# Where the adaLN blocks, the first three FFN blocks and the last sums stand in a two-layer diffusion trunk

## The chip, the cores and the metric

The kernel runs on one core of a Trainium2 chip. The metric is the device time of one execution in microseconds (us). Six actors matter: TensorE (PE, matrix products and transposes), VectorE (DVE), ScalarE (ACT), GpSimd (POOL), SyncE (SP), which issues nearly all transfers, and the transfer queues behind SP.

## The reference, cut to what matters

Two layers over 256 latent and 256 context tokens of width 1024: layer 0 mixes tokens with a Conformer convolution, layer 1 with retention; each is followed by a SwiGLU FFN. Every sub-layer is normalised, modulated by adaLN vectors (shift, scale, gate) and added back through its gate.

```python
def modulate(x, g, shift, scale):
    return rms_norm(x, g) * (1 + scale) + shift
...
def conv_module(h, w1, b1, dw, dw_b, norm_g, w2):
    ...
    y = jax.nn.silu(layer_norm(y, norm_g))
    return y @ w2
...
def swiglu_ffn(h, w_gu, w_down):
    a, b = jnp.split(h @ w_gu, 2, axis=-1)
    return (jax.nn.silu(a) * b) @ w_down
...
        x = x + g_m * ox
        x = x + g_f * swiglu_ffn(modulate(x, norm_ffn[i], sh_f, sc_f), ffn_w_gu[i], ffn_w_down[i])
```

## The kernel before, in words

**Products.** Everything is fp32, but PE works on pairs of shorter parts: each operand is split into a high part (`wh`, `ah`) and a low part (`wl`, `al`), and a product is three matmuls (`mm3`): high by high, low by high, high by low. A weight piece comes by a 1 MB load into a `raw` buffer, ACT copies its high part (128x1024), and DVE, or for some pieces POOL, subtracts to get the low part. `raw` buffers are shared by many loads, so a load waits for whatever read the buffer last. An activation is made of transposes on PE into one of two PSUM tiles called `aux`, a modulation on ACT or DVE, a CAST (high part) and a subtraction (low part) on DVE.

**The convolution's last product (`w2`).** `z` has eight chunks of 128 features. For each chunk ACT and DVE make `z`, and PE runs the 12 matmuls of chunk k into the four sums `w_00` to `w_03` (the tokens' four tiles, first 512 columns). Then come `w_10` to `w_13`, the other 512 columns, one tile after the other, each over all eight chunks. Their weights are the loads `w2_10` and `w2_11`. Between them stand pieces of the adaLN product: `begin(i)` is 16 matmuls (`ada`), `evict(i)` copies the sums on ACT (`adasb`), `cols(i)` is four matmuls on that copy, and `finish(i)` reduces on DVE. From block 4 the gate row is made (`gr` on PE, `grow` on ACT, `grd` to DRAM and two broadcast loads `gate` back); the residuals of `w_0*` and `w_1*` wait for `gate`.

**Residual, squares, norm.** `residual` is two DVE operations of 128x512 (times the gate, plus `res`); `squares` (`sqj`) on ACT sums their squares; `normed_sq` turns the sums of a pair of tiles into `rstd` (a chain of small DVE operations, some on 128x2, some on 128x1) and scales `res` to `xn`. `norm_parts` is a generator: each step transposes two features' tiles, modulates and splits them. Stream 0 (`x0`) are the first 256 tokens, stream 1 (`x1`) the others.

**FFN.** Block j of 22 makes `fa` and `fb` (128 hidden features each, 512 tokens) with 48 matmuls. Blocks 0 and 1 run in halves of 256 tokens, since `h` of stream 1 is not ready when they begin. From block 2 on, a `silu(a)*b` on ACT and DVE follows each block, and `fill_rows` loads and sums the adaLN columns of the next sub-layers (`adat`, `crow`, `junk`).

**The end.** In layer 1 the context is only read, so the last FFN has two token tiles and four sums `y`; each is multiplied by the gate, added to `res` and stored, the last one in two halves of 256 columns.

**What sets the order.** The instruction order of each engine is found by a scheduler at build time, except where `pin` holds it in the order of the code. Some pieces sit at places given by small tables (`T3_W2`, `CTX_AT`).

Of the kernel before, what the change touches and what calls it, by code (L numbers as in the profile page):

```python
# [82 lines left out]
def trunk_kernel(ctx: ExitStack, tc, x_in, ctx_in, cond, small, consts, rope, dist, ada, ada4, adat,  # L83
# [202 lines left out]
    def normed_sq(tiles, also=lambda i: None, act=False):  # L286
# [550 lines left out]
    for ch in range(KC):  # L837
# [21 lines left out]
        if ch == 4:  # L859
            begin(5)  # L860
            evict(5)
        if ch == 6:
            cols(5)
            finish(5)
    w2r[1, 1] = load(w2[1, 1], name="w2_11", also=pin)

    def w2_order(n):
        return ([(t, k) for k in range(KC) for t in range(4)] if n == 0
                else [(t, k) for t in range(4) for k in range(KC)])
# [4 lines left out]
    for t, k in w2_order(0):  # L874
        tk = slice(P * t, P * t + P)
        mm3(pw[t], (z[0][:, k, tk], z[1][:, k, tk]), w(k), k == 0, k == KC - 1)
        if k == KC - 1:
            residual(t, 0, pw[t], gates[t // 2])
            squares(t, 0, PAIRS[t // 2])
# [2 lines left out]
    ads = ExitStack()
    ad = ads.enter_context(tc.tile_pool(name="ad", bufs=1))

    crow = ad.tile([P, 2, D], F32, name="crow")
    for s in range(2):
        pin(nc.sync.dma_start(crow[:, s, :], cond[0:1, D * s:D * s + D].to_broadcast([P, D])))
        nc.scalar.activation(crow[:, s, :], crow[:, s, :], AF.Silu)
    junk = ad.tile([P, D], F32, name="junk")
# [22 lines left out]
    for n in (1,):  # L912
        pw = [acc(f"w2_{n}{t}") for t in range(4)]
        split_w2(n, 0)
        split_w2(n, 1)
        w = kview(w2p[n, 0] + w2p[n, 1], 512)
        for t, k in w2_order(n):
            tk = slice(P * t, P * t + P)
            last = pin if n and t > 1 else (lambda i: None)
            mm3(pw[t], (z[0][:, k, tk], z[1][:, k, tk]), w(k), k == 0, k == KC - 1, last)  # L920
            if k == KC - 1:
                residual(t, n, pw[t], gates[t // 2], last)
                squares(t, n, PAIRS[t // 2], last)
            if n and (t, k) == (1, KC - 1):
                mod_scale(0, 1)
                h = new_act(pB, "h0f")
                x0 = normed_sq(PAIRS[0], pin)
            if n and t == 3:
                if k == 0:
                    parts = norm_parts(0, 1, 0, x0, h, 0, pin, pin, range(1, 8, 2))  # L930
                if k in T3_W2:
                    next(parts)
# [7 lines left out]
    def gu_products(j, w, pa, pb, c0, c1, parts=None):  # L940
        for g, dst in enumerate((pa, pb)):
            c = slice(128 * g, 128 * g + 128)
            for k in range(KC):
                mm3(dst[:, c0:c1], w(k, c), (h[0][:, k, c0:c1], h[1][:, k, c0:c1]), k == 0, k == KC - 1,
                    pin if parts else lambda i: None)
                if parts and (g, k) in CTX_AT:
                    next(parts)
# [578 lines left out]
```

## Time and profile before

| what | value |
|---|---|
| median of 3 runs | 1071.44 us (1071.35 to 1071.82) |
| the profiled execution | 1070.6 us, its span 1068.8 us |
| TensorE's granted clock, mean | 1.00 |
| PE busy | 1053.4 us, 99% of the span |
| DVE / ACT / POOL busy | 690.3 / 412.2 / 161.4 us |
| chain that ended last | PE 92%, DVE 5%, ACT 1% |

A busy PE is in matmuls that overlap each other, so the time of one is read from start to start and not from its own duration. What can be won lies where PE waits for another engine, and at the two ends of the program.

### The profile page before, as it was taken

How to read it: one execution, taken by the hardware profiler on the slowest of the kernel's cores; microseconds unless marked ns; L12 is line 12 of the kernel's file. 1: busy time of each engine (PE TensorE's matmuls, PEld its weight loads, DVE VectorE, ACT ScalarE, POOL GpSimd, SP SyncE). 2: the span in 40 equal slices, each digit the busy share in tenths (PEclk: the TensorE clock that was granted, in tenths of full speed). 3: DMA queues.
4: the chain of work that ended last, by engine and by line, in shares of the span. 5: the costliest groups of instructions: out<-in, count | busy, mean ns of one | idle time of the engine just before them, and what ended most of it. 6: DMA issues, size and time to landing. Idle time of an engine off the chain costs nothing.

```text
span 1068.8 us, 13292 instructions
## 1 busy us (share of the span) xinstructions
PE 1053.4 (99%) x5214; PEld 841.2 (79%) x5214; DVE 690.3 (65%) x1163; ACT 412.2 (39%) x582; POOL 161.4 (15%) x120
## 2 busy tenths in 40 slices
PE   8999999989999999999999999999999999999998
PEld 4666745888888888888888888888888877888886
DVE  5598865768999886455746886457454565555545
ACT  4565455433222222222323563333332464444442
POOL 0079743030000000000002510000000470000000
PEclk9999999999999999999999999999999999999999
DMA  9567766724666685524132532235233353555551
GB/s 377 198 219 272 263 241 261 315 80 158 223 222 257 229 304 192 186 82 182 52 118 79 198 126 111 86 131 197 79 120 118 118 193 142 186 175 190 197 193 44
DMA packets 35037, 190.13 MB, mean 178 GB/s; under 512 B 3936, under 2 KB 4640, under 8 KB 15776
## 3 DMA queue, kind: packets, MB, share of 16 engines
q1 hardware_dynamic: 34544, 188.01, 48.6%
q10 hardware_dynamic: 432, 1.28, 0.3%
q8 instruction: 41, 0.67, 0.2%
q14 instruction: 20, 0.16, 0.0%
HBM read 185.85 MB, written 3.42 MB: 177 GB/s over the span
## 4 chain that ended last, share of the span: by engine, by line
PE 92%; DVE 5%; ACT 1%; issue 1%; DMA 0%; SPq 0%; ACTq 0%; DVEq 0%
PE fa L193 4%; PE fa L194 4%; PE fa L192 4%; PE fb L193 4%; PE fb L194 4%; PE fb L192 4%; PE u L194 3%; PE u L193 3%; PE u L192 3%; PE cv L529 3%; PE v L192 3%; PE v L194 3%; PE dn L192 3%; PE dn L193 3%; PE v L193 3%; PE dn L194 3%
## 5 line engine op out<-in xcount | busy, mean ns | idle before, releaser
L163 DVE TENSOR_TENSOR wl_gu<-raw_gu,wh_gu 128x1024 fp32r<-128x1024 f32 x76 | 92.3, 1223 | 78.9 <-ACT wh_gu L155 78.2
L155 ACT ACTIVATE wh_gu<-raw_gu 128x1024 fp32r<-128x1024 f32 x80 | 83.8, 1058 | 132.6 <-PE fb L193 47.9
L900 DVE SCALAR_TENSOR_TENSOR junk<-raw_adat,crow 128x1024 f32<-128x1024 f32 x80 | 97.7, 1222 | 0.9
L192 PE MATMUL fa<-ah_h0f,wh_gu 128*128 128x512 f32 (+1 forms) x192 | 71.5, 373 | 1.9 <-DVE ah_h0f L329 1.5
L163 DVE TENSOR_TENSOR wl_dn<-raw_dn,wh_dn 128x1024 fp32r<-128x1024 f32 x38 | 46.4, 1224 | 41.2 <-ACT wh_dn L155 41.0
L193 PE MATMUL fa<-al_h0f,wh_gu 128*128 128x512 f32 (+1 forms) x192 | 71.6, 373 | 0.2 <-DVE al_h0f L330 0.2
L192 PE MATMUL fb<-ah_h0f,wh_gu 128*128 128x512 f32 (+1 forms) x192 | 71.5, 373 | 0.0
L193 PE MATMUL fb<-al_h0f,wh_gu 128*128 128x512 f32 (+1 forms) x192 | 71.4, 372 | 0.0
L194 PE MATMUL fa<-ah_h0f,wl_gu 128*128 128x512 f32 (+1 forms) x192 | 71.3, 372 | 0.0
L194 PE MATMUL fb<-ah_h0f,wl_gu 128*128 128x512 f32 (+1 forms) x192 | 71.3, 372 | 0.0
L155 ACT ACTIVATE wh_dn<-raw_dn 128x1024 fp32r<-128x1024 f32 x38 | 40.2, 1061 | 77.5 <-PE dn L194 35.5
L163 POOL TENSOR_TENSOR wl_qk<-raw_qk,wh_qk 128x1024 fp32r<-128x1024 f32 x4 | 9.6, 2406 | 358.0 <-DVE res L364 346.1
L192 PE MATMUL u<-wh_gu,ah_h1f 128*128 128x512 f32 x156 | 61.5, 394 | 0.0
L194 PE MATMUL u<-wh_gu,al_h1f 128*128 128x512 f32 x156 | 60.7, 390 | 0.0
L193 PE MATMUL u<-wl_gu,ah_h1f 128*128 128x512 f32 x156 | 60.7, 390 | 0.0
L545 POOL TENSOR_TENSOR pacc<-pacc,pr 128x512 f32<-128x512 f32 x39 | 57.7, 1479 | 17.9 <-ACT pr L544 15.5
L562 DVE SCALAR_TENSOR_TENSOR lacc<-y,sm,lacc 128x512 f32<-128x512 f32 x65 | 49.1, 755 | 2.1
L193 PE MATMUL v<-wl_v,ah_h 128*128 128x512 f32 x128 | 50.0, 390 | 0.0
L192 PE MATMUL dn<-wh_dn,ah_hid 128*128 128x512 f32 x128 | 49.9, 390 | 0.0
L194 PE MATMUL v<-wh_v,al_h 128*128 128x512 f32 x128 | 49.9, 390 | 0.0
L194 PE MATMUL dn<-wh_dn,al_hid 128*128 128x512 f32 x128 | 49.8, 389 | 0.0
L193 PE MATMUL dn<-wl_dn,ah_hid 128*128 128x512 f32 x128 | 49.8, 389 | 0.0
(340 smaller groups left out, 2650.7 us busy)
## 6 DMA issues: line engine op xcount, KB each, us to landing
raw_gu<-in_gu_dram SPq DMA_DIRECT2D x44, 1024.0 KB, 4.8
raw_adat<-in_adat_dram SPq DMA_DIRECT2D x28, 1024.0 KB, 4.8
raw_dn<-in_dn_dram SPq DMA_DIRECT2D x19, 1024.0 KB, 4.7
raw_ada<-in_ada_dram SPq DMA_DIRECT2D x14, 1024.0 KB, 8.7
z<-yd SPq DMA_DIRECT2D x32, 284.5 KB, 4.0
raw_qk<-in_wqk_dram SPq DMA_DIRECT2D x8, 1024.0 KB, 4.7
raw_v<-in_wv_dram SPq DMA_DIRECT2D x8, 1024.0 KB, 4.8
raw_g<-in_wg_dram SPq DMA_DIRECT2D x8, 1024.0 KB, 4.8
```

The costliest lines, as they stand in the source:

```text
L155: also(nc.scalar.activation(hi[:, :m], raw[:, c:c + m], AF.Copy))
L163: also((eng or nc.vector).tensor_tensor(lo[:, :m], raw[:, c:c + m], hi[:, :m].bitcast(F32), op=ALU.subtract))
L192: also(nc.tensor.matmul(o, a[0], b[0], start=first, stop=False))
L193: also(nc.tensor.matmul(o, a[0], b[1], start=False, stop=False))
L194: also(nc.tensor.matmul(o, a[1], b[0], start=False, stop=last))
L529: pin(nc.tensor.matmul(cb[32 * q:32 * q + 32, :], dg[:, g, q, :], m, start=(g == 0), stop=(g == n - 1)))
L545: pin(nc.gpsimd.tensor_tensor(pacc, pacc, pr, op=ALU.add))
L562: pin(nc.vector.scalar_tensor_tensor(cacc, a, w, cacc, op0=ALU.mult, op1=ALU.add))
L900: pin(nc.vector.scalar_tensor_tensor(junk, raw[:, c, :], 1.0, crow[:, s, :], op0=ALU.mult, op1=ALU.mult, accum_out=mods[l][:, c0 + c, s:s ...
```

## The change

**Start.** The transposes and products of the last chunk move behind a part of the products of chunk 5, on PE only.

**`w2` and adaLN.** Blocks 4 and 5 leave the `z` loop and stand between the matmuls of `w_0*`. `w2_11` is now loaded ahead of the gate row's store, and the first FFN load `gu_0` ahead of the two gate loads. All of `w_1*` is pinned.

**FFN begin.** Three blocks (before: two) begin with stream 0 alone. The weights of block 0 have four buffers of their own, so that ACT and POOL split them before the norm of stream 0; blocks 0 to 2 get their low parts on POOL. Block 0 alternates `fa` and `fb`. The transposes of stream 1 stand in block 2's `fa`. `crow` and `adat` begin one block later.

**Norms.** In `normed_sq` the second sum (SCALAR_TENSOR_TENSOR) becomes one TENSOR_SCALAR for each tile; `x0`'s last half tile is scaled on ACT; `x1` wholly on ACT. `x0`'s modulation in layer 0 is all on ACT. In layer 1 odd features go to DVE, and the last norm and `tr1x` share their eight modulations anew.

**The last sums.** One of the four sums ends a block earlier and is folded into `res`; its last block goes to two sums of 256 columns. The other three are multiplied on DVE and added on POOL.

```diff
-CTX_AT = ((1, 3), (1, 4), (1, 6), (1, 7))
+CTX_AT = ((0, 1), (0, 3), (0, 5), (0, 7))
+T3_W2 = (0, 2, 4, 6)
+N_EARLY = 3
-T3_W2 = (0, 1, 5, 7)
...
-        also(nc.vector.scalar_tensor_tensor(a, ss[:, 1, 0:n], 1.0 / D, a, op0=ALU.mult, op1=ALU.add))
+        for i in range(n):
+            also(nc.vector.tensor_scalar(a[:, i:i + 1], ss[:, 1, i:i + 1], 1.0 / D, a[:, i:i + 1],
+                                         op0=ALU.mult, op1=ALU.add))
         rsqrt(a, rstd, n, also)
...
+            elif share and i == n - 1:
+                also(nc.scalar.activation(outs[i][:, 512:D], res[:, t, 512:D], AF.Identity, scale=rstd[:, i:i + 1]))
+                also(nc.vector.tensor_scalar(outs[i][:, 0:512], res[:, t, 0:512], rstd[:, i:i + 1], None, op0=ALU.mult))
...
+            if (f, p) == (KC - 3, 0):
+                start_T(KC - 1)
+                start_cols(KC - 1)
+                start_h(KC - 1)
...
-            begin(4)
-            evict(4)
-        if ch == 3:
-            cols(4)
-            finish(4)
+    w2r[1, 1] = load(w2[1, 1], name="w2_11", also=pin)
...
+        if (t, k) in ((3, 2), (3, 4)):
+            begin(3 + k // 2)
+            evict(3 + k // 2)
+        if (t, k) in ((3, 3), (3, 5)):
+            cols(3 + k // 2)
+            finish(3 + k // 2)
+        if (t, k) == (3, 3):
             gate_to_rows(0, 0, pin)
             gates = [gate_bc(0, 0, 0, pin), gate_bc(0, 0, 1, pin)]
...
+    split_w2(1, 0, also=pin)
+    split_w2(1, 1, also=pin)
+    for t in range(4):
+        residual(t, 0, pw0[t], gates[t // 2], pin)
+        squares(t, 0, PAIRS[t // 2], pin)
+    gu_raw = [load(gu0[j], name=f"gu0_{j}", also=pin) for j in range(N_EARLY)]
...
+        raw = gu_raw[j][:, 1024 * i:1024 * i + 1024]
+        pin(nc.scalar.activation(hi, raw, AF.Copy))
+        pin(nc.gpsimd.tensor_tensor(lo, raw, hi.bitcast(F32), op=ALU.subtract))
...
+    gu_piece(0, 0)
+    gu_piece(0, 1)
...
+            x0 = normed_sq(PAIRS[0], pin, share=True)
+            parts = norm_parts(0, 1, 0, x0, h, 0, pin, pin)
+    gu_piece(2, 0)
+    gu_piece(2, 1)
+    x1 = normed_sq(PAIRS[1], pin, act=True)
...
+        order = [(g, k) for g in range(2) for k in range(KC)]
+        if j == 0:
+            order.sort(key=lambda gk: gk[1])
...
-                            parts = norm_parts(1, 0, 0, x0, h, 0, pin)
+                            parts = norm_parts(1, 0, 0, x0, h, 0, pin, dve=range(1, 8, 2))
...
+                for f in range(4 * i, 4 * i + 4):
+                    if f % 4 < 2:
+                        pin(nc.scalar.activation(o, o, AF.Identity, scale=A, bias=B))
...
+                sums(py[t][n], t, c, j == 0, j == NB - 1 - t * n)
+                if last:
+                    finish_out(t, c, py[t][n], True)
+                elif t and n and j == NB - 2:
+                    residual(t, n, py[t][n], gate, pin)
...
+        pin(nc.vector.tensor_tensor(g, d, gate[:, c], op=ALU.mult))
+        pin((nc.gpsimd if share else nc.vector).tensor_tensor(res[:, t, c], g, res[:, t, c], op=ALU.add))
+        pin(nc.sync.dma_start(out[P * t:P * t + P, c], res[:, t, c]))
...
-    parts = norm_parts(1, 1, 0, x1, h, P, pin, dve=range(4, 8))
+    parts = norm_parts(1, 1, 0, x1, h, P, pin, dve=(2, 3, 6, 7))
```

SP's issues at the end of the `w2` stage, in the kernel before (`raw_w_10` and `raw_w_11` are the loads `w2_10` and `w2_11`):

```order
L145 DMA raw_w_10_1598<-in_w_dram 128x2048
L267 DMA grd_1652<-grow 16x128
L273 DMA gate_1654<-grd_1652 128x1024
L273 DMA gate_1656<-grd_1652 128x1024
L145 DMA raw_w_11_1693<-in_w_dram 128x2048
L887 DMA crow<-in_cond_dram 128x1024 x2
L145 DMA raw_gu_0_2048<-in_gu_dram 128x2048
```

and in the changed one:

```order
L143 DMA raw_w_10_1598<-in_w_dram 128x2048
L143 DMA raw_w_11_1647<-in_w_dram 128x2048
L265 DMA grd_1724<-grow 16x128
L143 DMA raw_gu_0_1840<-in_gu_dram 128x2048
L271 DMA gate_1726<-grd_1724 128x1024
L271 DMA gate_1728<-grd_1724 128x1024
L143 DMA raw_gu_1_1842<-in_gu_dram 128x2048
```

`raw_w_11` went from behind the gate row to ahead of it, and `raw_gu_0` from behind the gates to between the row's store and them.

ACT in the same stretch, before (`adasb` is an adaLN block's copy; `ah_z` and `zs` belong to `z`):

```order
L573 ACTIVATE adasb<-ada_1663 128x512
L841 ACTIVATE ah_z<-zt,sm 128x512
L842 ACTIVATE zs_1586<-zt,sm 128x512
L841 ACTIVATE ah_z<-zt,sm 128x512
L842 ACTIVATE zs_1585<-zt,sm 128x512
L155 ACTIVATE wh_w_10_1830<-raw_w_10_1598 128x1024
L155 ACTIVATE wh_w_10_1833<-raw_w_10_1598 128x1024
```

and in the changed kernel, from the copy of block 5 on:

```order
L581 ACTIVATE adasb<-ada_1742 128x512
L153 ACTIVATE wh_w_10_1806<-raw_w_10_1598 128x1024
L153 ACTIVATE wh_w_10_1809<-raw_w_10_1598 128x1024
L153 ACTIVATE wh_w_11_1814<-raw_w_11_1647 128x1024
L153 ACTIVATE wh_w_11_1817<-raw_w_11_1647 128x1024
L281 ACTIVATE sqj,ssq<-res 128x512 x4
L931 ACTIVATE wh_gu_00_1846<-raw_gu_0_1840 128x1024
L931 ACTIVATE wh_gu_01_1850<-raw_gu_0_1840 128x1024
L281 ACTIVATE sqj,ssq<-res 128x512 x2
L302 ACTIVATE xn<-res,rstd 128x512
```

All of `z` now lies ahead of block 5's copy, the high parts of `w_1*` stand directly behind it, and the two copies of the FFN's first weights stand between the squares of the first and of the second halves.

DVE at the norm of stream 0 in the changed kernel (`rs_a` and `rstd` are the small tiles of the chain):

```order
L368 TENSOR_TENSOR res<-w_11_1803,res 128x512
L294 TENSOR_SCALAR rs_a<-ssq,rs_a 128x1 x2
L199 TENSOR_SCALAR rstd<-rs_a 128x2
L200 TENSOR_SCALAR rs_h<-rs_a 128x2
L204 TENSOR_SCALAR rs_t<-rstd,rs_h 128x1 x2
L207 TENSOR_SCALAR rstd<-rs_t,rstd 128x1 x2
```

The first step was one SCALAR_TENSOR_TENSOR on 128x2; the two behind it are as they were.

## Rows read from the trace of the kernel before

**Rows 1.** The page: length of the span, busy time of each engine, and the chain that ended last by engine.

```profile
span 1068.8 us, 13292 instructions
...
PE 1053.4 (99%) x5214; PEld 841.2 (79%) x5214; DVE 690.3 (65%) x1163; ACT 412.2 (39%) x582; POOL 161.4 (15%) x120
...
PE 92%; DVE 5%; ACT 1%; issue 1%; DMA 0%; SPq 0%; ACTq 0%; DVEq 0%
```

**Rows 2.** PE's waits over the whole span: instruction that waited, the one that released it, us in total, times, the longest.

```profile
PE fa L192 <- DVE ah_h0f L329: 1.5, 2, 1.0
PE u L192 <- DVE ah_h1f L329: 1.3, 2, 1.1
...
PE tr L348 <- DVE al_h0f L330: 0.8, 2, 0.5
```

**Rows 3.** PE's timeline around the adaLN blocks 4 and 5 (start, busy us, instructions; in brackets the idle time before and what ended it).

```profile
172.66 1.92 PE L235 MATMUL ada<-raw_ada,csil 128*32 128x512 f32 x16
175.36 0.66 PE L240 MATMUL ada<-cst,adasb 128*128 128x128 f32 x4 [0.78 <-ACT adasb L573]
175.97 0.50 PE L192 MATMUL w<-wh_w,ah_z 128*128 128x512 f32 x1
...
182.18 0.64 PE L235 MATMUL ada<-raw_ada,csil 128*32 128x512 f32 x4 [0.35 <-ACT grow L265]
```

**Rows 4.** SP's timeline in that stretch, and two groups of transfers: the gate's in that stretch and, from the page, the 1 MB loads of the FFN (KB each, median us from issue to landing).

```profile
182.15 0.34 SPq L267 DMA_DIRECT2D grd<-grow  x1
186.06 0.81 SPq L273 DMA_DIRECT2D gate<-grd  x2
186.98 0.37 SPq L145 DMA_DIRECT2D raw_w<-in_w_dram  x1
...
gate<-grd SPq DMA_DIRECT2D x2, 512.0 KB, 4.6
...
raw_gu<-in_gu_dram SPq DMA_DIRECT2D x44, 1024.0 KB, 4.8
```

**Rows 5.** Timelines of ACT (two rows) and of DVE (four) between the `w2` stage and the norm of stream 0.

```profile
195.36 1.06 ACT L155 ACTIVATE wh_w<-raw_w 128x1024 fp32r<-128x1024 f32 x1 [5.00 <-DMA raw_w<-in_w_dram]
...
208.31 0.63 ACT L283 ACTIVATE sqj<-res 128x512 f32<-128x512 f32 x1 [0.61 <-DVE res L364]
...
188.25 1.23 DVE L163 TENSOR_TENSOR wl_w<-raw_w,wh_w 128x1024 fp32r<-128x1024 f32 x1
...
197.59 1.89 DVE L363 TENSOR_TENSOR w<-w,gate 128x512 f32<-128x512 f32 x3
...
209.53 0.46 DVE L206 TENSOR_SCALAR rs_t<-rstd,rs_h 128x1 f32<-128x1 f32 x2
...
211.38 1.41 DVE L301 TENSOR_SCALAR xn<-res,rstd 128x1024 f32<-128x1024 f32 x2
```

**Rows 6.** PE's timeline from the first transposes of stream 0 to FFN block 3 (248.45 is the first matmul of block 2, 259.35 that of block 3).

```profile
212.51 0.88 PE L348 MATMUL tr<-cst,xn 128*128 128x128 f32 x4
...
217.68 0.36 PE L192 MATMUL fa<-ah_h0f,wh_gu 128*128 128x256 f32 x1 [0.40 <-POOL wl_gu L163]
...
224.64 0.28 PE L194 MATMUL fb<-ah_h0f,wl_gu 128*128 128x256 f32 x1
225.96 0.39 PE L192 MATMUL fa<-ah_h0f,wh_gu 128*128 128x256 f32 x1 [1.04 <-DVE ah_h0f L329]
...
232.31 0.60 PE L348 MATMUL tr<-cst,xn 128*128 128x128 f32 x4
...
236.05 0.63 PE L348 MATMUL tr<-cst,xn 128*128 128x128 f32 x4 [0.52 <-DVE al_h0f L330]
...
248.33 0.28 PE L194 MATMUL fb<-ah_h0f,wl_gu 128*128 128x256 f32 x1
248.45 0.40 PE L192 MATMUL fa<-ah_h0f,wh_gu 128*128 128x512 f32 x1
...
259.35 0.39 PE L192 MATMUL fa<-ah_h0f,wh_gu 128*128 128x512 f32 x1
```

**Rows 7.** Timelines of DVE and of POOL at two places where small steps of a norm ran while POOL made low parts: at 571 to 574 (one POOL row, one DVE row) and at 877 to 883 (one POOL row, two DVE rows).

```profile
570.98 2.42 POOL L163 TENSOR_TENSOR wl_qk<-raw_qk,wh_qk 128x1024 fp32r<-128x1024 f32 x1 [346.14 <-DVE res L364]
...
572.62 0.80 DVE L293 TENSOR_SCALAR rs_a<-ssq 128x2 f32<-128x2 f32 x1
...
877.86 4.76 POOL L163 TENSOR_TENSOR gu_11vl<-raw_gu,gu_11vh 128x1024 fp32r<-128x1024 f32 x2
...
880.06 0.14 DVE L293 TENSOR_SCALAR rs_a<-ssq 128x1 f32<-128x1 f32 x1
880.94 1.70 DVE L294 SCALAR_TENSOR_TENSOR rs_a<-ssq,rs_a 128x1 f32<-128x1 f32 x1 [0.73 <-ACT sqj L283]
```

**Rows 8.** PE's first product of the last FFN, and ACT's scaling of the last norm.

```profile
875.49 0.50 PE L192 MATMUL u<-gu,ah_h1f 128*128 128x512 f32 x1 [1.09 <-DVE ah_h1f L329]
...
884.80 1.33 ACT L299 ACTIVATE xn<-res,rstd 128x512 f32<-128x512 f32 x2 [2.88 <-DVE rstd L209]
```

**Rows 9.** The end: DVE's last operation, SP's five stores of the output, and from the page POOL's sums of 128x512 (busy us, mean ns of one).

```profile
1065.28 0.42 DVE L364 TENSOR_TENSOR res<-y,res 128x256 f32<-128x256 f32 x1
...
1061.26 4.80 SPq L1367 DMA_DIRECT2D out_dram<-res  x5
...
L545 POOL TENSOR_TENSOR pacc<-pacc,pr 128x512 f32<-128x512 f32 x39 | 57.7, 1479 | 17.9 <-ACT pr L544 15.5
```

More of the change, by code (lines that the diff above doesn't have):

```diff
@@ L284, in squares, with normed_sq @@
                                   accum_out=ssq[tiles][:, n, i:i + 1]))
[L286 removed]
+    def normed_sq(tiles, also=lambda i: None, act=False, share=False):
         n = len(tiles)
@@ L470, in trunk_kernel @@
             start_sums(f + 2)
-        if more:
+        if more and f + 1 < KC - 1:
             if f:
@@ L851, in trunk_kernel @@
             finish(3)
-            begin(4)
-            evict(4)
-        if ch == 3:
-            cols(4)
-            finish(4)
+    w2r[1, 1] = load(w2[1, 1], name="w2_11", also=pin)
+    pw = [acc(f"w2_0{t}") for t in range(4)]
+    w = kview(w2p[0, 0] + w2p[0, 1], 512)
+    for t, k in [(t, k) for k in range(KC) for t in range(4)]:
+        tk = slice(P * t, P * t + P)
+        mm3(pw[t], (z[0][:, k, tk], z[1][:, k, tk]), w(k), k == 0, k == KC - 1)
+        if (t, k) in ((3, 2), (3, 4)):
[5 more added lines that the diff above has]
+        if (t, k) == (3, 3):
             gate_to_rows(0, 0, pin)
             gates = [gate_bc(0, 0, 0, pin), gate_bc(0, 0, 1, pin)]
[L859 to L869, printed above, removed]
-    pw = [acc(f"w2_0{t}") for t in range(4)]
-    w = kview(w2p[0, 0] + w2p[0, 1], 512)
[L874 to L879, printed above, removed]
+    pw0 = pw
     cvs.close()
     pB = ctx.enter_context(tc.tile_pool(name="pB", bufs=1))
[L882 to L889, printed above, removed]
+    gxs = ExitStack()
+    gx = gxs.enter_context(tc.tile_pool(name="gx", bufs=1))
     def ada_next(i):
@@ L906, in trunk_kernel, with rows_begin @@
     adr = list(range(28))
+    ads = ExitStack()
+    def rows_begin():
+        ad = ads.enter_context(tc.tile_pool(name="ad", bufs=1))
+        crow = ad.tile([P, 2, D], F32, name="crow")
+        for s in range(2):
+            nc.sync.dma_start(crow[:, s, :], cond[0:1, D * s:D * s + D].to_broadcast([P, D]))
+            nc.scalar.activation(crow[:, s, :], crow[:, s, :], AF.Silu)
+        return ad, crow, ad.tile([P, D], F32, name="junk")
     def fill_rows(n):
@@ L910, in fill_rows @@
             ada_next(adr.pop(0))
[L912 to L932, printed above, removed]
@@ new lines, in trunk_kernel @@
+    gu_piece(0, 0)
+    gu_piece(0, 1)
+    for t in range(4):
+        tk = slice(P * t, P * t + P)
+        for k in range(KC):
+            mm3(pw[t], (z[0][:, k, tk], z[1][:, k, tk]), w(k), k == 0, k == KC - 1, pin)
+            if t == 3 and k in T3_W2:
+                next(parts)
+        if t == 3:
+            gu_piece(1, 0)
+            gu_piece(1, 1)
+            squares(2, 1, PAIRS[1], pin)
+        residual(t, 1, pw[t], gates[t // 2], pin)
+        if t != 2:
+            squares(t, 1, PAIRS[t // 2], pin)
+        if t == 1:
+            mod_scale(0, 1)
+            h = new_act(pB, "h0f")
+            x0 = normed_sq(PAIRS[0], pin, share=True)
+            parts = norm_parts(0, 1, 0, x0, h, 0, pin, pin)
@@ L940, in gu_products @@
     def gu_products(j, w, pa, pb, c0, c1, parts=None):
[L941 to L947, printed above, removed]
+        order = [(g, k) for g in range(2) for k in range(KC)]
+        if j == 0:
+            order.sort(key=lambda gk: gk[1])
+        for g, k in order:
+            mm3((pa, pb)[g][:, c0:c1], w(k, slice(128 * g, 128 * g + 128)), (h[0][:, k, c0:c1], h[1][:, k, c0:c1]),
+                k == 0, k == KC - 1, pin if j < N_EARLY else lambda i: None)
+            if parts and (g, k) in CTX_AT:
+                next(parts)
     early = []
@@ L1352, in down, with sums, finish_out @@
         w = kview(ahead or weights(dn1[j], name=f"dn1_{j}"), 1024)
+        last = j == NB - 1
+        def sums(o, t, c, first, stop):
+            tk = slice(P * t, P * t + P)
+            for k in range(2):
+                mm3(o, (hid[0][:, k, tk], hid[1][:, k, tk]), w(k, c), first and k == 0, stop and k == 1, also)
         for t in range(2):
[L1354 removed]
             for n in range(2):
[L1356 to L1367 removed]
+                if t and n and last:
+                    for c in range(512, D, OUT_W):
+                        d = acc(f"yl{c}")[:, 0:OUT_W]
+                        sums(d, t, slice(c, c + OUT_W), True, True)
+                        finish_out(t, slice(c, c + OUT_W), d)
+                    continue
+                c = slice(512 * n, 512 * n + 512)
+                sums(py[t][n], t, c, j == 0, j == NB - 1 - t * n)
[3 more added lines that the diff above has]
+                    residual(t, n, py[t][n], gate, pin)
+    def finish_out(t, c, d, share=False):
+        g = t2("yg")[:, 0:c.stop - c.start] if share else d
+        pin(nc.vector.tensor_tensor(g, d, gate[:, c], op=ALU.mult))
+        pin((nc.gpsimd if share else nc.vector).tensor_tensor(res[:, t, c], g, res[:, t, c], op=ALU.add))
+        pin(nc.sync.dma_start(out[P * t:P * t + P, c], res[:, t, c]))
     uw = {}
```

50 lines of the change are left out of this document (21 added, 29 removed).

## The prediction

> **What bounds the kernel now.** First the page's busy times and the chain of waits [rows 1]: PE is busy for 99% of the span and holds 92% of the chain, so time can only come from its own instructions, from the few places where it waits, and from the tail. Then PE's waits over the span [rows 2] and its timeline where they lie [rows 3, 6]: most belong to the stretch from 172 to 236 us (the adaLN blocks 4 and 5, then the norm in front of the first FFN), one of about 1.1 to the last FFN's start [rows 8]; behind the last matmul DVE and SP's stores run alone [rows 9]. The reader is to see that each wait is short, a few tenths to 1.1 us, and ends with a split on DVE, a copy on ACT or a low part from POOL. So the change can win single microseconds, and each place where it puts a wait of its own costs as much. About 0.2%, 2.1 us, is what a measurement of this kernel can tell from no change.
>
> **Start.** Only PE's order changes. Chunk 7's parts come through ACT and DVE in the order that they had, so its products find them when they did: 0, and at most 0.1 either way.
>
> **The adaLN blocks and w2.** Before, block 4's begin, its columns and the next product start at 172.66, 175.36 and 175.97 [rows 3]. Its 16 matmuls are 1.85 from start to start and four columns 0.1 more than a wait would leave, so 3.31 less 1.95 gives 1.36 lost; in front of block 5's begin PE idles 0.35 for the gate row's copy. Both go, since products now stand between: -1.7. What comes in their place I count from 172.66 with 0.227 a matmul of 512 columns (48 of them from 248.45 to 259.35 [rows 6]). Two begins are 3.7, the 70 matmuls of chunks 2 to 7 ahead of block 5's end 15.9, block 4's columns and the gate row 0.6: block 5 ends at 192.9. Columns came 0.85 behind the begin's end before, 175.36 against 172.66 + 1.85 [rows 3]; two matmuls cover 0.45 of it: wait 0.3 to 0.4. The high part of w_10's first piece stands behind block 5's copy on ACT and takes 1.06, its low part 1.23 behind that [rows 5]: ready at 194.7 and 196.0. Before, both were made while z still ran; now PE waits 0.6 for the one and, with one matmul between, 1.1 for the other. Load w2_11 waits until block 5's begin has read the shared buffer, about 192.0; 4.8 to land as the 1 MB loads do [rows 4], 1.06 and 1.23 for its parts: 199.1, where PE stands at 198.7: 0.4 to 0.5. New waits 2.4, old ones 1.7: **+0.7**. PE comes to the first transposes of stream 0 at 213.2 in place of 212.51 [rows 6].
>
> **What SP's wait holds back.** Queued behind w2_11 on SP are the gate row's store, gu_0 and the two gates, and all of layer 0's residuals wait for the gates. Store at 192.4; the gates follow 3.9 later, 182.15 to 186.06 before, and land 4.6 after that [rows 4]: 201.0, against 190.7 before. PE does not feel this at once (w_10 to w_13 run until 218), the norm does. Eight residual steps at 0.63 (three in 1.89 [rows 5]) end at 206.0, and ACT's fourth square 1.0 later, at 207.0. Then ACT makes both high parts for gu_0 (209.1) and the two squares of w_10 and w_11 (0.63 and its read, 1.5 for two [rows 5]): 210.6. DVE's first small steps reach the 128x2 ones at 211.0.
>
> **The held step.** POOL starts gu_0's low parts at 208.1, two in a row at 2.38 each (4.76 for two [rows 7]), until 212.9. Before, no norm of stream 0 ran beside POOL. Where one did, rows 7 show what happens: a TENSOR_SCALAR of 128x2 at 572.62 took 0.80 and ended at 573.42 when POOL's piece ended (570.98 + 2.42 = 573.40); a 128x1 at 880.06 took 0.14 in the middle of POOL's piece; a SCALAR_TENSOR_TENSOR of 128x1 with two inputs took 1.70, until 882.64, with POOL's end at 882.62. The change replaces that last kind by 128x1 TENSOR_SCALARs, which go free, but the next two steps of stream 0's chain stay 128x2. One of them is an integer step that no row shows beside POOL; the other has the kind, type and shape of the row at 572.62. Bounds: 0 and POOL's rest, 212.9 less 211.0 = 1.9. I take 1.9, since that row is the nearest. By the Trainium skill ("SBUF — State Buffer", section "Who interferes with whom") a TENSOR_SCALAR that streams one SBUF tensor through both DVE ports and a GpSimd instruction shut each other out for a whole instruction, whoever starts first. By that the integer step is held too, and the sum is the same. The row at 572.62 agrees: 0.80.
>
> **The FFN's begin.** From 212.9: two 128x2 steps 0.35, the twelve single steps 1.85 (209.53 to 211.38), xn 0.7 and its half 0.4 [rows 5]; first transposes at 216.3, where PE waits since 213.2: 3.1. Then PE has the other 21 matmuls of w_13 (4.8), 16 transposes with their restarts (1.8), three first halves of 48 at 0.12 (17.3; 0.12 is 248.33 to 248.45 [rows 6]), stream 1's transposes (1.8) and three second halves (17.3). Block 2 in halves is 96 x 0.12 against 48 x 0.227, +0.6, and is in this. One wait is new: stream 1's third transposes need the `aux` tile of its first, which came free 3.7 after the first began (232.31 to 236.05 [rows 6]); only six matmuls and the second transposes stand between now, 2.3, so 1.4, and 0.1 at the fourth. Waits that go: DVE's and POOL's at 217.68, 225.96 and 236.05 [rows 2, 6], about 4.1 with the restarts. Block 3 starts at 216.3 + 44.5 = 260.8, before 259.35: **+1.45** for w2 and FFN begin together. Without the hold it would be 258.9, -0.45. Behind it crow, the copies for gu_3 and the adaLN sums start a block later; ACT and DVE have them some 3 us ahead of PE, so I cost them at nothing; without that cover each us late costs one.
>
> **Layer 1.** Odd features on DVE in stream 0's modulation: the two engines take turns on one tile, +0.1. At the last FFN's start the first tile's split now comes first: 0.33 of the 1.09 [rows 8]. In the last norm the 1.70 step [rows 7] becomes 0.14, but ACT's scaling at 884.80 [rows 8] then finds ACT busy with the hidden parts, so 0.2 of 1.5 shows, and the two modulations on DVE bring the split 0.5 earlier, of which a half stays. **-0.6**, bounds -0.9 and 0.
>
> **The tail.** DVE ended at 1065.70, the last store's issue at 1066.06, the span at 1068.8 [rows 9]. With three adds off DVE its last step ends near 1065.0. But POOL needs 1.48 for each add [rows 9], the third ends near 1064.7, and three stores of about 0.4 are issued behind it, in order: the last at 1065.5 to 1065.9. **-0.3**, bounds -0.7 and +0.3.
>
> **Sum.** +1.45 + 0.1 - 0.6 - 0.3 = +0.7 (0.65) on the profiled execution's 1070.6: 1071.3. That execution lies 0.8 under the median, its span 1068.8 with 1.8 around it; the difference is what carries over: 1071.44 + 0.7 = **1072.1**.
>
> **Rivals.**
> - *Not held.* POOL's second piece starts later or the 128x2 steps slip between. -1.9: 1070.2. For it: the place depends on when the gates land; earlier gates shift both alike, against it. Chance 0.20.
> - *More is won.* The hold is absent or short, and stream 1's transposes don't wait (1.5), with layer 1 and the tail at their good bounds: 1070.2 - 1.6 = 1068.6. For it: my waits behind the moved loads are built from medians. Chance 0.15.
> - *Slower: the loads behind SP's wait.* w2_11 took from 186.98 to 195.36 [rows 4, 5], 8.4, when gates and others shared the queues. Now the store and gu_0 share them. At 8.4 PE waits 3.6 longer in w_10, hence 1072.1 + 3.6 = 1075.7. It turns to slower from 1.5 over my 4.8. If only the gates come late, each us is one at the norm. Against it: the two gates were issued ahead of it then [rows 4], now nothing is. Chance 0.17.
> - *The waits only move.* Block 5 stands at the end of w_0*, so its copy delays w_1*'s weights: that is in the forecast at 2.4 against 1.7.
>
> **How the numbers follow.** The forecast has 0.48, with 1070.4 to 1073.9 as its own range (gates 1 us either way, layer 1 and tail at their bounds). Faster, under 1069.3: nearly all of the second rival and a quarter of the first, 0.20. Slower, over 1073.6: the third and an eighth of the forecast, 0.22. Within: 0.58. The range 1068.6 to 1074.6 leaves half of the second rival and somewhat over half of the third outside.
>
> **What would show it.** In the changed profile: w_10's first matmuls wait about 0.6 and 1.1; the gates land near 201; a 128x2 step of the norm lasts near 2 us and ends with POOL's second low part of gu_0; the first transposes follow near 216.3, block 3 near 260.8; stream 1's third transposes wait 1.4; the span from block 3 to layer 1 is as before; the last store is issued near 1065.7. Gates landing past 203, or a wait at gu_3 to gu_5, would make the forecast wrong on the slow side; first transposes before 214.5 on the fast side.

## The result, and the profile after

The changed kernel takes 1075.8 us (median of 7 runs, 1074.53 to 1077.96) against 1072.51 for the kernel before (7 runs, 1071.35 to 1074.31): ratio 1.0035, interval 1.0022 to 1.0048, or 3.75 us at its middle (the two medians lie 3.3 apart). It is slower, by more than a measurement's 0.2%, and it lies 1.2 us above the upper end of the forecast's range. The forecast counted from 1071.44, the median of the first 3 runs of the kernel before; so the step to judge it by is +3.75 against its +0.65, and not 1075.8 against 1072.1.

Two executions of the changed kernel were profiled. The first is the slowest of its runs (1077.96), and 3.0 us of its lead over the trace of before (by how much the same instruction comes later) arise ahead of the `w2` stage, in the convolution, where the change touches nothing; the nine other profiles show 0.2 to 3.1 there, this very kernel 0.2 in its second one (`e8_changed_again`, 1074.7). The rows below come from that second profile, in which the end of the convolution lies at +0.16 us, so that times can be laid beside those of before.

Its page, the rows that answer to [rows 1]:

```profile
span 1072.9 us, 13411 instructions
...
PE 1056.9 (99%) x5268; PEld 846.7 (79%) x5268; DVE 690.2 (64%) x1162; ACT 415.5 (39%) x587; POOL 169.3 (16%) x125
...
PE 92%; DVE 4%; DMA 2%; ACT 1%; issue 1%; SPq 0%; ACTq 0%; DVEq 0%
```

PE is as busy as before in share, and 3.5 us longer in sum, though by the forecast only block 2's halves add work, 0.6. PE's waits over the span, against [rows 2]:

```profile
PE tr L352 <- DVE xn L305: 3.2, 3, 2.7
...
PE tr L352 <- DVE al_h0f L334: 1.2, 1, 1.2
...
PE w L191 <- DVE wl_w L161: 0.9, 1, 0.9
...
PE w L190 <- ACT wh_w L153: 0.3, 1, 0.3
```

The waits of `fa` are gone, one of 2.7 for the normed stream has come, and one of 1.2 at stream 1's third transposes. The integer step of the norm of stream 0, as DVE ran it in the kernel before, with POOL idle:

```profile
209.26 0.17 DVE L201 TENSOR_SCALAR rstd<-rs_a 128x2 int32<-128x2 int32 x1
```

DVE's, POOL's, ACT's and SP's timelines there in the changed kernel, one fence each:

```profile
201.45 0.70 DVE L367 TENSOR_TENSOR w<-w,gate 128x512 f32<-128x512 f32 x1 [0.88 <-DMA gate<-grd]
...
211.09 2.41 DVE L199 TENSOR_SCALAR rstd<-rs_a 128x2 int32<-128x2 int32 x1
```

```profile
208.72 4.76 POOL L932 TENSOR_TENSOR wl_gu<-raw_gu,wh_gu 128x1024 fp32r<-128x1024 f32 x2 [36.40 <-ACT wh_gu L931]
```

```profile
186.90 0.27 ACT L263 ACTIVATE grow<-gr 16x128 f32<-16x128 f32 x1 [5.29 <-PE gr L261]
```

```profile
192.50 0.33 SPq L143 DMA_DIRECT2D raw_w<-in_w_dram  x1
192.92 0.38 SPq L265 DMA_DIRECT2D grd<-grow  x1
...
197.49 0.80 SPq L271 DMA_DIRECT2D gate<-grd  x2
```

The gates are issued at 197.49, where they were at 186.06 [rows 4], since the row's store now stands behind the load that waits for a buffer: ACT had the row ready at 187.17, and the store went out at 192.92, right behind `w2_11`. DVE begins its residuals with them at 201.45. The 128x2 integer step starts at 211.09 and ends at 213.50, when POOL's second piece ends (208.72 + 4.76 = 213.48). So the chain that was forecast is there, to half a microsecond. PE's timeline, against [rows 3, 6]:

```profile
195.02 0.50 PE L190 MATMUL w<-wh_w,ah_z 128*128 128x512 f32 x1 [0.29 <-ACT wh_w L153]
...
196.42 0.51 PE L191 MATMUL w<-wl_w,ah_z 128*128 128x512 f32 x1 [0.90 <-DVE wl_w L161]
...
199.50 0.50 PE L191 MATMUL w<-wl_w,ah_z 128*128 128x512 f32 x1
...
216.58 1.30 PE L352 MATMUL tr<-cst,xn 128*128 128x128 f32 x4 [2.73 <-DVE xn L305]
...
218.53 0.63 PE L192 MATMUL w<-wh_w,al_z 128*128 128x512 f32 x1
218.95 0.63 PE L190 MATMUL w<-wh_w,ah_z 128*128 128x512 f32 x1
...
222.75 0.39 PE L191 MATMUL w<-wl_w,ah_z 128*128 128x512 f32 x1
222.98 0.39 PE L192 MATMUL w<-wh_w,al_z 128*128 128x512 f32 x1
...
226.17 0.28 PE L190 MATMUL fa<-ah_h0f,wh_gu 128*128 128x256 f32 x1
...
264.05 0.40 PE L190 MATMUL fa<-ah_h0f,wh_gu 128*128 128x512 f32 x1
```

The first transposes start at 216.58, 0.3 from the forecast. Behind them the matmuls of `w_13` start 0.42 to 0.43 apart (218.53 to 218.95), and only from 222.75 on 0.23 apart. The table by stretches of the same kernel (busy us and instructions of PE, PEld, DVE, ACT, POOL, then the granted clock, DMA share and GB/s) says why. Its levels 1.00 and 0.50 are 2.4 and 1.2 GHz.

```profile
210.00:214.00 4.00, 3.84 (x17) 2.83 (x16) 3.30 (x7) 0.81 (x4) 3.48 (x2) 1.00 0.00 0
214.00:216.00 2.00, 0.00 (x0) 0.00 (x0) 1.77 (x12) 0.42 (x1) 0.00 (x0) 0.96 0.80 213
216.00:218.00 2.00, 1.42 (x5) 1.21 (x6) 1.97 (x4) 0.39 (x2) 0.00 (x0) 0.50 0.75 315
218.00:220.00 2.00, 2.00 (x6) 1.52 (x6) 1.16 (x3) 0.99 (x2) 0.00 (x0) 0.50 0.00 0
220.00:222.00 2.00, 2.00 (x9) 1.60 (x8) 0.47 (x1) 0.64 (x2) 0.00 (x0) 0.50 0.00 0
222.00:224.00 2.00, 2.00 (x11) 1.68 (x10) 1.38 (x2) 0.59 (x2) 0.00 (x0) 0.83 0.00 0
224.00:226.00 2.00, 2.00 (x13) 1.65 (x12) 0.98 (x2) 1.25 (x3) 0.00 (x0) 1.00 0.03 8
```

The granted clock is 1.00 until PE's wait and 0.50 behind it, for some 6 us. PE counts as busy there, so neither the waits nor the busy share shows this loss. The first profile shows the same behind a wait of 4.0, for about 3 us:

```profile
220.00:222.00 2.00, 1.02 (x5) 0.82 (x6) 1.86 (x4) 0.74 (x2) 0.00 (x0) 0.93 0.96 406
222.00:224.00 2.00, 2.00 (x6) 1.54 (x5) 1.52 (x3) 0.97 (x2) 0.00 (x0) 0.50 0.02 8
224.00:226.00 2.00, 2.00 (x9) 1.66 (x9) 0.45 (x1) 0.66 (x2) 0.00 (x0) 0.71 0.00 0
```

The tail of the second profile (DVE, POOL, SP), against [rows 9]:

```profile
1069.06 0.42 DVE L1408 TENSOR_TENSOR res<-yl,res 128x256 f32<-128x256 f32 x1
```

```profile
1065.13 4.06 POOL L1408 TENSOR_TENSOR res<-yg,res 128x512 f32<-128x512 f32 x3 [177.56 <-DVE yg L1407]
```

```profile
1066.46 4.07 SPq L1409 DMA_DIRECT2D out_dram<-res  x5
```

From block 3 on the lead falls: +4.70 at block 3's start, +4.74 at the last matmul's, +3.78 at DVE's end, +4.1 at the span's.

### The profile page after: what moved, and what is told of

Its sections match the earlier page's. It is cut to its first block, busy times and chain, and to the rows that moved or that the text cites. A ratio compares the mean times of both kernels' runs of the same rounds, so it can differ in the third digit from the quotient of the medians.

```text
span 1076.1 us, 13411 instructions
## 1 busy us (share of the span) xinstructions
PE 1057.5 (98%) x5268; PEld 844.5 (78%) x5268; DVE 690.1 (64%) x1162; ACT 415.6 (39%) x587; POOL 169.4 (16%) x125
## 4 chain that ended last, share of the span: by engine, by line
PE 89%; DVE 4%; DMA 3%; ACT 2%; POOL 1%; issue 1%; SPq 0%; ACTq 0%; POOLq 0%; DVEq 0%
PE u L192 4%; PE fb L190 4%; PE fb L191 4%; PE fb L192 4%; PE u L190 4%; PE fa L190 4%; PE fa L191 4%; PE fa L192 4%; PE u L191 4%; PE v L191 3%; PE v L190 3%; PE dn L190 3%; PE dn L191 3%; PE v L192 3%; PE dn L192 3%; PE g L190 2%
## 5 line engine op out<-in xcount | busy, mean ns | idle before, releaser
L161 DVE TENSOR_TENSOR wl_gu<-raw_gu,wh_gu 128x1024 fp32r<-128x1024 f32 x74 | 89.8, 1223 | 76.3 <-ACT wh_gu L153 75.3
L153 ACT ACTIVATE wh_gu<-raw_gu 128x1024 fp32r<-128x1024 f32 x74 | 77.5, 1057 | 120.7 <-PE fb L191 45.6
```

Of the source, the lines that this page charges most:

```text
L153: also(nc.scalar.activation(hi[:, :m], raw[:, c:c + m], AF.Copy))
L161: also((eng or nc.vector).tensor_tensor(lo[:, :m], raw[:, c:c + m], hi[:, :m].bitcast(F32), op=ALU.subtract))
```

## The experiments

Theory: the time went to PE's wait at the first transposes, which the held step makes, and to the halved clock behind it. Rivals: the late gates make the wait whatever POOL does; the loss lies in the other parts of the change; the clock is a coincidence of one profile. Ratios are against the kernel before on the same chip; the changed kernel's is 1.0031 to 1.0035.

**`e1_single_steps`: the held steps taken apart, all else as changed.**

```diff
-        also(nc.vector.tensor_scalar(y.bitcast(I32), a.bitcast(I32), -0.5, 1597463007.0, op0=ALU.mult, op1=ALU.add))
-        also(nc.vector.tensor_scalar(nh, a, -0.5, None, op0=ALU.mult))
+        for i in range(n):
+            also(nc.vector.tensor_scalar(y[:, i:i + 1].bitcast(I32), a[:, i:i + 1].bitcast(I32), -0.5, 1597463007.0,
+                                         op0=ALU.mult, op1=ALU.add))
+        for i in range(n):
+            also(nc.vector.tensor_scalar(nh[:, i:i + 1], a[:, i:i + 1], -0.5, None, op0=ALU.mult))
```

> The changed kernel with the two 128x2 steps of the norm's chain split into steps of 128x1. Theory (those steps are held by POOL's second low part of gu_0, and the long wait of PE then also costs its clock): the step of 2.39 us shrinks to about 0.2, the first transposes of stream 0 come 2.2 us earlier, PE's wait there falls from 4.0 to 1.9 us, the granted clock stays at 1.00 behind it, and the time is about 4 us under the changed kernel, level with the kernel before (-0.3 us). If the hold counts but the clock doesn't: 2.1 us under the changed kernel, +1.6 against before. Rival (the hold lies beside other work): no change, +3.7 against before.

Measured 1071.56 against 1071.71: 0.9999 (0.9990 to 1.0008). The whole loss of 3.75 is gone. DVE's and then PE's timelines:

```profile
213.26 0.27 DVE L200 TENSOR_SCALAR rstd<-rs_a 128x1 int32<-128x1 int32 x2
213.45 0.20 DVE L203 TENSOR_SCALAR rs_h<-rs_a 128x1 f32<-128x1 f32 x2
```

```profile
198.25 0.49 PE L191 MATMUL w<-wl_w,ah_z 128*128 128x512 f32 x1 [0.90 <-DVE wl_w L161]
...
216.78 0.60 PE L355 MATMUL tr<-cst,xn 128*128 128x128 f32 x4
...
223.38 0.28 PE L190 MATMUL fa<-ah_h0f,wh_gu 128*128 128x256 f32 x1
...
261.26 0.40 PE L190 MATMUL fa<-ah_h0f,wh_gu 128*128 128x512 f32 x1
```

POOL's pieces run from 210.55 to 215.31 here, over all four single steps, whose busy times add up to 0.47. PE doesn't wait at the transposes, its granted clock stays 1.00 behind them, and from there to the first `fa` it needs 6.60, where the changed kernel needed 226.17 - 216.58 = 9.59 and, in its first profile, 8.55. The difference is 1.9 to 3.0. Not all of it is the clock: behind a wait PE needs 6.97 at a clock of 1.00 too (`e2`), so the clock's part is 2.6 in the one and 1.6 in the other.

A halved clock is in this profile too, at another place, as a line of its table by stretches shows:

```profile
200.00:202.00 2.00, 2.00 (x6) 1.55 (x5) 1.86 (x2) 1.05 (x2) 0.00 (x0) 0.50 0.99 403
```

It fell behind `w_10`'s waits of 0.29 and 0.90 and was back at 1.00 before 204. From 198.25 to the transposes PE took 18.5, where the second profile took 17.3 (196.42 to 213.7), and that delay is in part why PE doesn't wait at 216.78. Six other profiles (both of the changed kernel, `e2`, `e3`, `e5`, `e6`) have the same two waits and a clock of 1.00 behind them.

**`e2_gates_first`: `w2_11` loaded behind the gates again.**

```diff
-    w2r[1, 1] = load(w2[1, 1], name="w2_11", also=pin)
...
             gates = [gate_bc(0, 0, 0, pin), gate_bc(0, 0, 1, pin)]
+            w2r[1, 1] = load(w2[1, 1], name="w2_11", also=pin)
```

> The changed kernel with one issue of SP moved: load w2_11 behind the two gate loads, as it was before. Theory (the gates are late because SP stands still for w2_11's buffer): the gate row is stored about 5.5 us earlier and the gates land near 6 us earlier, while w2_11 is issued when it was, since the gates wait for the row; the norm of stream 0 then waits for w_11's own residual, its 128x2 steps come when POOL is through, PE's wait of 4.0 us goes and the clock stays: 5 to 6 us under the changed kernel, about 2 under the kernel before; if w2_11 lands later behind the gates, up to 2 us of that are lost at w_10. Rival (only the hold matters, not the gates): the hold moves along and 1.9 us of wait stay, 2 to 4 us under the changed kernel. Rival (neither): +3.7 against before.

Measured 1073.05 against 1071.71: 1.0014 (1.0005 to 1.0023). The rival was right about the hold: the gates were issued at 188.69, 8.8 earlier, but on DVE the residuals then stood behind the low parts of `w_11`, until 201.23, and the whole chain, POOL's pieces too (208.49 to 213.25), lay where it had been. DVE's and PE's timelines:

```profile
211.03 2.25 DVE L199 TENSOR_SCALAR rstd<-rs_a 128x2 int32<-128x2 int32 x1
```

```profile
216.35 0.95 PE L352 MATMUL tr<-cst,xn 128*128 128x128 f32 x4 [1.77 <-DVE xn L305]
```

So with the gates early and `w2_11` behind them the hold stays; `e7` has both early, and `e9` both early with the 128x2 steps. What fell was PE's wait, to 1.77, since PE came later by a wait of 0.68 for a low part of `w_11`, and behind it the clock stayed 1.00: 216.35 to 223.32 (the first `fa`) is 6.97. So 1.8 to 2.2 us came off, near the rival's 2 to 4, where the theory wanted 5 to 6.

**`e3_filled_wait`: the wait kept, PE kept busy in it** with 14 matmuls into a sum that nobody reads.

```diff
+            if (t, k) == (3, 0):
+                fill = acc("fill")
+                for _ in range(14):
+                    pin(nc.tensor.matmul(fill, z[0][:, 0, tk], w(0)[0], start=True, stop=True))
```

> The changed kernel with 14 matmuls of 512 columns (3.2 us, into a sum that nobody reads) in PE's wait ahead of stream 0's first transposes. Theory (the clock fell because PE stood idle): the transposes start when they did, the clock behind them stays at 1.00, and the 1.9 us that seven matmuls and three groups of transposes lost at half the clock come back: 1.9 us under the changed kernel, +1.8 against before. Rival (the matmuls behind the wait are slow for another reason): no change, +3.7; if the wait is shorter than 3.2 us in other executions: slower by the difference.

Measured 1073.74 against 1071.71: 1.0021 (1.0012 to 1.0030), 1.1 to 1.5 us under the changed kernel by the ratios, whose intervals overlap a little. The step is held as before (214.30, 2.41). PE's timeline, and a line of the table by stretches:

```profile
216.72 3.34 PE L944 MATMUL fill<-wh_w,ah_z 128*128 128x512 f32 x14
219.89 0.83 PE L352 MATMUL tr<-cst,xn 128*128 128x128 f32 x4
...
226.74 0.28 PE L190 MATMUL fa<-ah_h0f,wh_gu 128*128 128x256 f32 x1
```

```profile
218.00:220.00 2.00, 2.00 (x11) 1.50 (x9) 1.77 (x7) 0.73 (x1) 0.00 (x0) 1.00 0.82 328
```

The clock is 1.00 throughout, and 219.89 to 226.74 is 6.85, not 9.59. PE was given 14 matmuls more and is not slower for it. So a part of the loss is the clock behind the wait and not the wait itself: 9.59 - 6.85 = 2.7 by the second profile, 8.55 - 6.85 = 1.7 by the first. The times alone, with intervals that overlap, would not show it.

**`e4_without_w2_ffn`: the rest of the change alone** (start loop, norms, layer 1, tail; `w2` and the FFN's begin as before).

```diff
-        also(nc.vector.scalar_tensor_tensor(a, ss[:, 1, 0:n], 1.0 / D, a, op0=ALU.mult, op1=ALU.add))
+        for i in range(n):
+            also(nc.vector.tensor_scalar(a[:, i:i + 1], ss[:, 1, i:i + 1], 1.0 / D, a[:, i:i + 1],
+                                         op0=ALU.mult, op1=ALU.add))
...
-                            parts = norm_parts(1, 0, 0, x0, h, 0, pin)
+                            parts = norm_parts(1, 0, 0, x0, h, 0, pin, dve=range(1, 8, 2))
...
+                elif t and n and j == NB - 2:
+                    residual(t, n, py[t][n], gate, pin)
```

> The kernel before with the rest of the change alone: start loop, norms, layer 1's modulation, last norm and last sums; the w2 stage and FFN begin as before. Theory (all that was lost was lost in w2 and FFN begin): 0.7 to 1.0 us under the kernel before. Rival (the 3 us that the changed kernel's trace shows ahead of the end of the convolution belong to the start loop's new order): 2 to 3 us over the kernel before.

Measured 1071.95 against 1071.71: 0.9999 (0.9990 to 1.0007). In its trace the stretch from the first `w` product to DVE's end is 0.67 shorter than before (its lead is +0.66 at the one and -0.01 at the other), as forecast; the times can't show so little. The loss is not in these parts.

**`e5_pool_piece_later`: POOL's second piece behind the norm's small steps,** which stay 128x2.

```diff
     gu_piece(0, 0)
-    gu_piece(0, 1)
...
             x0 = normed_sq(PAIRS[0], pin, share=True)
+            gu_piece(0, 1)
```

> The changed kernel with the second piece of gu_0 (its copy on ACT and its low part on POOL) moved behind the norm of stream 0; the norm's steps stay 128x2. Theory (POOL's second low part is what holds them): POOL's first piece ends about when the step begins, so the step takes under 0.4 us, and the result is that of the split steps: 3 to 4 us under the changed kernel, within 1 us of the kernel before. Rival (the 128x2 form itself is slow there, whatever POOL does): the step keeps over 2 us and the time stays at +3.7 against before. If the second piece is then late for block 0: a new wait of PE at fa of block 0.

Measured 1072.47 against 1071.91: 0.9999 (0.9990 to 1.0008). The same step, with only the second piece's copy on ACT and its low part on POOL moved (POOL's and DVE's timelines):

```profile
211.92 2.41 POOL L932 TENSOR_TENSOR wl_gu<-raw_gu,wh_gu 128x1024 fp32r<-128x1024 f32 x1 [37.44 <-ACT wh_gu L931]
...
218.18 2.40 POOL L932 TENSOR_TENSOR wl_gu<-raw_gu,wh_gu 128x1024 fp32r<-128x1024 f32 x1 [3.85 <-ACT wh_gu L931]
```

```profile
213.84 0.52 DVE L199 TENSOR_SCALAR rstd<-rs_a 128x2 int32<-128x2 int32 x1
```

The step takes 0.52, where I expected under 0.4, and ends at 214.36, with POOL's first piece (214.33). It is POOL that holds it, and for as long as POOL's instruction has still to run. PE waits 1.35, and its clock stays 1.00 behind it.

**`e6_split_and_spread`: `e1`, and stream 1's transposes spread over two blocks.**

```diff
-CTX_AT = ((0, 1), (0, 3), (0, 5), (0, 7))
+CTX_AT = ((0, 1), (0, 3), (1, 2), (1, 4))
```

> The split steps (128x1), and stream 1's third and fourth transposes seven matmul groups later in block 2. Theory (the third waits 1.2 us for the PSUM tile of the first): that wait goes, 1.3 us under the split steps alone, so 1.3 to 1.5 under the kernel before. Rival (the split of stream 1 is then late for the second halves): a wait of up to 1 us at block 0's second half, no gain.

Measured 1070.12 against 1071.91: 0.9982 (0.9973 to 0.9991). By the ratios that is 1.8 under `e1`, whose interval it touches; the wait of 1.2 at the third transposes is gone, so the forecast's term for it was right.

**`e7_blocks_earlier`: `e6`, blocks 4 and 5 and the gates earlier.** `w_0*` is pinned, block 5 begins ahead of block 4's columns, and the row's store goes ahead of `w2_11`.

```diff
-    w2r[1, 1] = load(w2[1, 1], name="w2_11", also=pin)
...
-        mm3(pw[t], (z[0][:, k, tk], z[1][:, k, tk]), w(k), k == 0, k == KC - 1)
+        mm3(pw[t], (z[0][:, k, tk], z[1][:, k, tk]), w(k), k == 0, k == KC - 1, pin)
...
-        if (t, k) in ((3, 3), (3, 5)):
-            cols(3 + k // 2)
-            finish(3 + k // 2)
-        if (t, k) == (3, 3):
+        if (t, k) in ((3, 4), (3, 6)):
+            cols(2 + k // 2)
+            finish(2 + k // 2)
+        if (t, k) == (3, 4):
             gate_to_rows(0, 0, pin)
+            w2r[1, 1] = load(w2[1, 1], name="w2_11", also=pin)
```

> The kernel of the split steps and spread transposes, and in the w2 stage the matmuls held in the order of the code: block 5 begins behind chunk 4, block 4's columns stand behind it, block 5's behind chunk 6, and w2_11 is loaded between the gate row's store and the gates. Theory (the 2.3 us lost between block 5's begin and w_10 come from block 5 standing at the end of w_0): those waits go and the gates land some 5 us earlier, 2 us under the kernel without this, 3 to 4 under the kernel before. Rival (the waits come from elsewhere, z or the loads): a new wait at block 5's begin or within the chunks takes 1 us or more of it back.

Measured 1067.45 against 1071.91: 0.9950 (0.9936 to 0.9963), 5.4 us, the fastest of all and faster than both kernels. SP's timeline:

```profile
189.36 0.34 SPq L268 DMA_DIRECT2D grd<-grow  x1
189.81 0.36 SPq L143 DMA_DIRECT2D raw_w<-in_w_dram  x1
...
190.73 1.12 SPq L274 DMA_DIRECT2D gate<-grd  x2
```

Block 5's begin now starts at 185.81 (191.37 in the changed kernel), the gates are issued 6.8 earlier, and PE waits neither at `w_10` nor at the first transposes (small new waits are 0.78 at 169.46 for a block's copy and 0.44 at 188.76 for the gate row). I expected 3 to 4; which of its edits gave the rest was not separated.

**`e8_changed_again`: the changed kernel, once more.**

> The changed kernel as it is, for a second profile and a second interval: over the kernel before by 3.0 to 4.5 us. If the long wait ahead of stream 0's transposes is again 2.5 us or more and the granted clock falls to 0.5 behind it, the clock is part of the usual cost; if the wait is shorter and the clock stays, the first profile was an unlucky one and the hold and the late gates are the whole cost.

Measured 1075.68 against 1072.11: 1.0031 (1.0022 to 1.0040), and the profile shown above. The halved clock behind the first transposes is in both profiles of this kernel; in `e1` to `e3`, `e5` to `e7` and `e9` the granted clock is 1.00 in each stretch from 214 to 222. (Elsewhere it is not: `e1` has 0.50 at 200 to 202, `e5` and `e7` at 16 to 18.)

So two profiles could still be chance. But each run's mean granted clock is on record too, and it answers for all of them: 0.9972 over the 18 runs of the changed kernel, 0.9993 over 68 runs of the kernel before, 0.9984 in `e1`, 0.9983 in `e2`, 0.9990 in `e3`, 0.9997 in `e4`. With PE busy for 99% of the span, a run at a mean of 0.9972 loses, as an estimate, 0.0028 of its 1073 us, 3.0 us, and the kernel before 0.7: some 2.3 of the 3.75 are the clock. In `e1` 1.8 are still lost to it.

**`e9_earlier_still_held`: `e7` with the 128x2 steps back** (the lines of `e1` undone).

> The best kernel so far (blocks earlier, spread transposes) with the 128x2 steps back. Theory (the hold costs what PE has no work for): the step is held for 2 us or more again, the first transposes wait 1 to 2 us, and the time is 1 to 2 us over that kernel, still 2 to 3 under the kernel before. Rival (earlier gates alone cure it, so that the hold lies beside other work): level with that kernel, 5.4 us under the kernel before.

Measured 1068.21 against 1072.11: 0.9963 (0.9949 to 0.9976). DVE's and PE's timelines:

```profile
210.14 0.97 DVE L199 TENSOR_SCALAR rstd<-rs_a 128x2 int32<-128x2 int32 x1
```

```profile
214.18 0.94 PE L352 MATMUL tr<-cst,xn 128*128 128x128 f32 x4 [0.48 <-DVE xn L305]
```

POOL's pieces ended at 211.08, sooner than I had thought, so the step was held 0.97 and not over 2, and PE waited 0.48. The intervals of this run and of `e7` overlap: the 1.4 between them is a middle, and what makes more of it than the 0.48 of waiting was not followed. The same source lines cost 3.8 us in one order of work and some 1.4, not clear of the noise, in another.

## Why the prediction was wrong

It forecast +0.65 and +3.75 came. By its own steps, with the second profile's times less the 0.16 that the convolution left:

- *The adaLN blocks and w2* (+0.7). The old waits went. At `w_10` PE idles 0.29 and 0.90; counted from start to start, as the forecast was, it loses near 0.55 and 1.17 there (0.6 and 1.1 forecast; 195.02 to 196.42 is 1.40, less 0.227), and 0.22 at the load `w2_11`'s first low part (199.05 to 199.50, less 0.227; 0.4 to 0.5 forecast). PE issues its last product ahead of the transposes at 213.45 and could go on at 213.7: 213.5 against 213.2 forecast. Right within 0.3.
- *What SP's wait holds back.* The gate row is stored at 192.92 (192.4), the gates follow 4.57 later (3.9) and DVE uses them 3.96 after that (4.6): 201.45 (201.0). The two errors cancel. Right.
- *The held step* (1.9). 2.41 in a step that took 0.17 in the trace of before, hence 2.2; the end is POOL's end to 0.02. The row of [rows 7] that I took for the nearest was the right one, for the integer step too. The Trainium skill ("SBUF — State Buffer", section "Who interferes with whom") has the two engines shut each other out for a whole instruction where DVE streams one tensor through both of its ports; the 2.41 here and the 0.52 of `e5` agree. The 128x1 steps of `e1`, 0.27 for two, were not held.
- *The FFN's begin: the step that failed.* "First transposes at 216.3, where PE waits since 213.2" was right: 216.4. "Block 3 starts at 216.3 + 44.5" was not: 264.05 - 216.58 = 47.5, so 3.0 are missing. The 44.5 itself was counted rightly: in `e1`, without a wait and at a clock of 1.00, it is 261.26 - 216.78 = 44.48. I priced everything behind the wait at the durations of a PE that had not waited (0.227 a matmul of 512 columns). After 2.73 us without work the granted clock was 0.50, and the matmuls came 0.42 to 0.43 apart until 222.4. The missing term is what PE loses behind the wait, 3.0 in this profile and 1.9 in the first: some 0.4 for starting again, as in `e2`, and for the rest, 2.6 and 1.6, the clock's price. `e3` shows it with the hold and without the idle PE; the mean clock of all runs puts it at 2.3. The Trainium skill ("TensorE: Matmul & The Clock Gate", section "What's actually happening") states the two levels and that idleness brings the lower; the 0.50 behind 2.73 us without work agrees. The prediction did not ask whether its own 3.1 us of waiting falls under that.
- *Stream 1's third transposes* (1.4). 1.25 at 242.11, 1.2 in `e1`, and nothing in `e6`. Right.
- *Layer 1* (+0.1 - 0.6). +0.36 by the first product of v, then -0.32 up to the last matmul: 0.0 from block 3 to there. The gain at the last FFN's start was 0.28 (a wait of 0.8 for 1.09 [rows 8]); the last norm gave 0.22 and lost 0.17 again. The forecast was too good by 0.5, which is the bad end of its bounds.
- *The tail* (-0.3). DVE ends 0.96 sooner behind the last matmul, the span 0.6. Better than forecast by 0.3; POOL's third add ends at 1069.19, ahead of DVE's last (1069.48), and the stores' queue ends 4.07 after 1066.46, at 1070.53, so the span gains less than DVE.

The forecast's size plus the missing 3.0 gives +3.65, and +3.75 was measured; that this comes so close is partly luck, since layer 1 (0.5 too good) and the tail (0.3 too cautious) nearly cancel. The rival that ended slower named 1075.7, close to the result, but for a cause that isn't there: it wanted `w2_11` to take 8.4, and its parts began 4.6 after its issue (192.50 to 197.12). *Not held* would have been worth 1.9 by that count; `e1` shows 3.8, since a step that is not held takes away PE's whole wait and a part of the clock's price (3.0 to 1.8 by the mean clocks). The rival *More is won* was added up wrongly: 1.5 and the good bounds, 0.3 and 0.4, come to 2.2 and not to 1.6, so 1068.0; nothing here hangs on it. A range that had priced the wait at both levels of the clock would have reached 1075.1 and above.

## What to carry to other kernels

The price of a wait on TensorE is its length and what the granted clock does behind it, so a wait is to be read together with the clock of the stretches behind it, and closing a part of it may win more than that part (`e2`: 1.0 less of waiting, 1.8 to 2.2 us less in all). Its length alone does not tell whether the clock falls. The 128x2 steps of one input here waited until GpSimd's instruction ended (0.52 to 2.41), and the 128x1 steps did not: taking such steps apart by column, or moving GpSimd's piece, is to be tried before anything larger. And in one queue everything stands behind the load that waits for a buffer: the small store that starts a chain belongs ahead of it. What that is worth by itself was not measured here; `e7` does it together with other edits.
